# Cosine-similarity attention on one core: norm sums of later pairs attached one turn earlier, with new orders on three engines

## The chip, the core and the metric

The kernel runs on one core of a Trainium2 chip. The metric is the device time of one execution in microseconds. The core has five engines that run on their own and meet at semaphores: TensorE (PE in the profile, with its weight loads as PEld), VectorE (DVE), ScalarE (ACT), GpSimd (POOL) and SyncE (SP), which issues nearly all DMAs here. Each engine works through a list of instructions of its own.

## The reference

```
batch, heads, seq, dim = 8, 12, 512, 64          # Q, K, V in float32, tau = 0.1
Q_norm = Q / (norm(Q, axis=-1) + 1e-10)
K_norm = K / (norm(K, axis=-1) + 1e-10)
scores = einsum('bhqd,bhkd->bhqk', Q_norm, K_norm) / tau
weights = exp(scores - max(scores, -1));  weights /= sum(weights, -1) + 1e-10
out = einsum('bhqk,bhkd->bhqd', weights, V)
```

There are 96 heads. For each, the rows of Q and K are scaled to length one, a 512 x 512 matrix of scores is formed, its exponential is taken, and the weighted mean of the rows of V goes out. The kernel leaves the maximum away, as scores of unit vectors are bounded.

## The kernel before

The 96 heads are worked on as 48 **pairs**, numbered 0 to 47; the work on one pair in the steady state is a **turn**. For each pair s the function `pair` and its inner `rest` add small operations to a list, each with a name, an engine and the operations that it needs. The names and lines that matter:

- **Squares** `("SQ", s, 0)` (line 366): GpSimd squares all of Q and K of the pair into bfloat16. A few early ones are split (lines 254 to 357).
- **Norm sums** `("SSQ", s, w)` (line 395): TensorE adds up the squares with eight matmuls against the identity matrix, once for Q (w = 0) and once for K. They write into spare columns, from 320 on, of one of the two PSUM banks in which value products stand. Because of this a norm sum is *attached* to one half of the value products of an earlier pair, (i, h): it runs behind the last value group of that half, the reciprocal of that half waits for it too, and the next value products in the bank wait until its result has been read. Lines 209 to 229 choose the attachment: they go through the pairs in the order of a due time, `due_red`, and give each the first free half whose slot is not before it.
- **Norm reduce** `("RED", s, 1)` (line 404): VectorE reduces the sums of a pair to 128 x 16 squared norms. Four pairs (35, 39, 43, 47) are reduced by VectorE straight from the squares (line 412).
- **Root** `("NEW", g, k)` (lines 437 to 467): pairs are grouped in ones, twos and, from pair 20 on, fours. For each group a chain of eight or nine small VectorE steps makes the inverse roots out of the squared norms. For the first groups ScalarE does it.
- **Scale** `("SCL", s, w)` (line 479): Q (w = 0) and K (w = 1) times the inverse root, to bfloat16. VectorE does all of Q and 30 of the pairs' K, GpSimd the others' K.
- **Transpose** `("TR", s, w)` (line 488, TensorE, four matmuls) and **copy** `("EVA", s)` (line 506, VectorE), which brings the transposed pair out of PSUM.
- **Score product** `("SCO", s, c)` (line 625): two matmuls of 512 columns for chunk c, 0 to 3, of the keys. There are two PSUM places, so a score product waits for the exponential two before it.
- **Exponential** `("EXP", s, c)` (line 649): ScalarE, 128 x 1024 elements. In pairs 33, 40 and 46 the last chunk is not done by ScalarE: VectorE (lines 567, 569) and GpSimd (six steps, lines 589 to 595) work it out as a polynomial.
- **Cast** `("VC", s)` (line 657): GpSimd turns V into bfloat16.
- **Value product** `("PV", s, h, i)` (line 674): four matmuls, eight such groups for a pair, one bank for each head h. **Reciprocal** (line 690) and **normalise** (line 692) on VectorE empty the bank, and the next pair's products of that head wait for it. Then SyncE stores the result. The last pair's products have lines of their own (708 to 725).

What order the engines follow is not worked out when the program is built. `ORDER` at the end of the file holds, for each engine, a list of operation numbers, written out: number n is the n-th operation that was added. `schedule` (line 33) turns the lists into programs. `run` (line 43) puts a wait in front of an operation for what it needs from other engines. The due times (`due_sq`, `due_red` and others), the kinds of operation and constants such as START and PERIOD come from the planner that once wrote the lists. In this file only the attachment of norm sums still depends on them.

Some numbers that are used later: 663 is the scale of pair 16's K on GpSimd, 768 and 845 the squares of pairs 19 and 21, 708, 674 and 1831 the casts of pairs 17, 16 and 47; 846 and 847 the norm sums of pair 21; 666, 820, 1069, 1150, 1212, 1255 and 1410 score products (16,0), (20,0), (27,1), (29,3), (31,0), (32,0) and (36,0); 931 and 1225 value products (23,0,0) and (31,1,0); 906 and 1198 the normalisations (22,0) and (30,1); 1333 the copy of pair 34, 1363 a transpose of pair 35; 1790 to 1795 the six polynomial steps of pair 46 on GpSimd.

## Time and profile before

| | |
|---|---|
| median of 3 runs | 190.72 us (190.54 to 191.19) |
| the profiled execution | 190.63 us |
| its span, first to last instruction | 188.7 us |
| TensorE busy | 180.1 us, 95% |
| ScalarE busy | 181.0 us, 96% |
| VectorE busy | 167.8 us, 89% |
| GpSimd busy | 167.5 us, 89% |
| granted TensorE clock, mean | 0.997 |
| moved between HBM and the core | 50.79 MB |

The profile shows one execution. A row of its groups names line, engine and operation, what is written and read, the shapes, a count, busy time, the mean of one in ns, and the idle time of the engine ahead of it with what ended it. The chain of waits goes back from the last instruction, at each step to what released it. A timeline lists the instructions of one engine by start and length, neighbours of one kind merged; a bracket behind a row is idle time ahead of it. In a merged row the length runs from the first start to the last end. Instructions of an engine overlap by their pipelines, so that the start of the next is a better measure of a price than the length of one.

### The profile page before, as it was taken

What the parts mean: (1) busy time and instruction counts of PE and PEld (TensorE: products, weight loads), DVE (VectorE), ACT (ScalarE), POOL (GpSimd) and SP (SyncE); (2) the same over time, 40 slices, a digit from 0 to 9 for tenths busy, and PEclk for the clock granted to TensorE, in tenths of its full rate; (3) what the DMA queues carried; (4) which work ended last, traced back from release to release, by engine and by line L of the source; (5) the groups of instructions that cost most, each with busy time, mean ns of one, the idle gap of its engine ahead of it and who ended that gap; (6) DMA issues with size and microseconds to landing.
All of it is one profiled execution on the core that took longest, in us unless ns stands there. A gap on an engine that the chain in (4) does not pass through costs nothing.

```text
span 188.7 us, 7244 instructions
## 1 busy us (share of the span) xinstructions
PE 180.1 (95%) x3009; PEld 117.3 (62%) x3009; DVE 167.8 (89%) x539; ACT 181.0 (96%) x209; POOL 167.5 (89%) x143
## 2 busy tenths in 40 slices
PE   7899999999999999999999999999999999899993
PEld 2456666666666676677666665666577556455662
DVE  2788999999999988997979999999999999999654
ACT  5799999999999999999999999999999999999992
POOL 3699899979899899299999998989999999998980
PEclk9999999999999999999999999999999999999998
DMA  4999999999999998999999998974999540113335
GB/s 151 331 350 351 348 357 330 285 326 362 382 380 379 302 287 263 273 347 361 379 380 344 297 307 283 293 221 148 280 376 348 158 162 13 46 63 108 111 115 168
DMA packets 52448, 50.79 MB, mean 269 GB/s; under 512 B 3136, under 2 KB 52416, under 8 KB 52416
## 3 DMA queue, kind: packets, MB, share of 16 engines
q1 hardware_dynamic: 51984, 50.02, 80.7%
q8 instruction: 23, 0.38, 0.8%
q10 hardware_dynamic: 432, 0.33, 0.5%
q14 instruction: 9, 0.07, 0.1%
HBM read 37.75 MB, written 12.58 MB: 267 GB/s over the span
## 4 chain that ended last, share of the span: by engine, by line
PE 67%; DVE 16%; ACT 12%; DMA 1%; issue 1%; POOL 0%; DVEq 0%
PE oops L674 23%; PE scps L625 23%; ACT et L649 12%; PE tps L488 10%; PE oops L395 9%; DVE ob L692 3%; DVE qt L506 3%; DVE qn L479 2%; DMA qk<-in_K_dram 1%; DVE rd L690 1%; DVE nps L437 1%; DVE xp L567 1%; DVE nps L404 1%; DVE xz L569 1%; DVE xs L260 1%
## 5 line engine op out<-in xcount | busy, mean ns | idle before, releaser
L649 ACT ACTIVATE et<-scps 128x1024 bf16<-128x1024 f32 (+1 forms) x190 | 174.6, 1049 | 0.8 <-PE scps L625 0.4
L366 POOL TENSOR_TENSOR sq<-qk 128x1024 bf16<-128x1024 f32 x44 | 82.7, 1893 | 1.0 <-DMA qk<-in_K_dram 1.0
L625 PE MATMUL scps<-qt 64*128 64x512 bf16 x378 | 74.5, 386 | 1.3 <-ACT et L649 0.7
L674 PE MATMUL oops<-vb,et 128*128 128x65 bf16 x1504 | 74.5, 194 | 0.8 <-DVE ob L692 0.2
L674 PEld LDWEIGHTS oops<-vb,et 128*128 128x128 bf16 x1504 | 56.1, 98 | 30.6 <-issue 18.1
L479 DVE TENSOR_TENSOR qn<-qk,nps 128x512 bf16<-128x512 f32 x77 | 50.7, 676 | 0.6 <-ACT nps L429 0.6
L692 DVE TENSOR_TENSOR ob<-oops,rd 128x256 f32<-128x256 f32 x94 | 38.9, 418 | 1.3 <-DVE rd L690 0.2
L488 PE MATMUL tps<-ident,qn 128*128 128x128 bf16 x376 | 33.8, 220 | 0.8 <-DVE ys L437 0.4
L506 DVE COPY qt<-tps 128x1024 bf16<-128x1024 bf16 x47 | 32.1, 682 | 0.7 <-PE tps L488 0.5
L395 PE MATMUL oops<-sq,ident 128*128 128x64 bf16 x688 | 31.0, 193 | 0.5 <-POOL sq L357 0.5
L657 POOL TENSOR_SCALAR vb<-vf 128x512 bf16<-128x512 f32 x48 | 29.3, 626 | 0.3
L488 PEld LDWEIGHTS tps<-ident,qn 128*128 128x128 bf16 x376 | 21.6, 98 | 10.6 <-issue 4.3
L395 PEld LDWEIGHTS oops<-sq,ident 128*128 128x128 bf16 x688 | 24.3, 98 | 6.0 <-issue 4.3
L625 PEld LDWEIGHTS scps<-qt 64*128 64x128 bf16 x378 | 18.2, 92 | 14.7 <-ACT et L649 2.4
L479 POOL TENSOR_TENSOR qn<-qk,rk 128x512 bf16<-128x512 f32 x17 | 17.7, 1042 | 8.0 <-DVE rd L690 4.1
L690 DVE RECIPROCAL rd<-oops 128x4 f32<-128x4 f32 x94 | 15.8, 174 | 7.0 <-PE oops L674 4.6
L404 DVE TENSOR_REDUCE nps<-oops 128x16 f32<-128x128 f32 x40 | 11.4, 286 | 2.7 <-PE oops L395 2.6
L437 DVE SCALAR_TENSOR_TENSOR nps<-nps,ys 128x32 f32<-128x32 f32 (+3 forms) x48 | 8.3, 192 | 0.5
L590 POOL TENSOR_TENSOR xw<-xw,xz 128x1024 f32<-128x1024 f32 x3 | 7.1, 2356 | 0.3
L595 POOL TENSOR_TENSOR xz<-xz,xw 128x1024 f32<-128x1024 f32 x3 | 7.1, 2354 | 0.2
L590 POOL TENSOR_TENSOR xw<-xz 128x1024 f32<-128x1024 f32 x3 | 5.7, 1894 | 1.0 <-DVE xz L569 1.0
L590 POOL TENSOR_TENSOR et<-xw,xp 128x1024 bf16<-128x1024 f32 x3 | 6.4, 2126 | 0.2
(62 smaller groups left out, 75.2 us busy)
## 6 DMA issues: line engine op xcount, KB each, us to landing
vf<-in_V_dram SPq DMA_DIRECT2D x48, 256.0 KB, 6.1
qk<-in_Q_dram SPq DMA_DIRECT2D x47, 256.0 KB, 4.9
qk<-in_K_dram SPq DMA_DIRECT2D x47, 256.0 KB, 6.2
out_dram<-ob SPq DMA_DIRECT2D x47, 256.0 KB, 3.9
qk<-in_Q_dram SPq DMA_DIRECT2D x2, 128.0 KB, 2.6
qk<-in_K_dram ACTq DMA_DIRECT2D x2, 128.0 KB, 2.8
out_dram<-ob SPq DMA_DIRECT2D x1, 128.0 KB, 1.8
out_dram<-ob ACTq DMA_DIRECT2D x1, 64.0 KB, 1.7
```

The costliest lines, as they stand in the source:

```text
L366: lambda e: e.tensor_tensor(out=sqf, in0=data, in1=data, op=ALU.mult))
L395: last = e.matmul(out=o_ps[bank][:, at : at + 64], lhsT=ident[:, :], rhs=sq[iqs][:, 8 * w : 8 * w + 8, 8 * k : 8 * k + 8], start=(k == 0), ...
L479: lambda e, w=w, r=r: e.tensor_tensor(out=qn[iqn][:, w].rearrange("p t h d -> p h t d"), in0=qk[iq][:, w].rearrange("p h (t d) -> p h t d" ...
L488: last = e.transpose(t_ps[:, w, t, :], qn[iqn][:, w, t].rearrange("p h d -> p (h d)"), ident[:, :])
L506: lambda e, ws=ws: e.tensor_copy(out=qt[iqt][:, ws, :, :].rearrange("p w t x -> p (w t x)"), in_=t_ps[:, ws, :, :].rearrange("p w t x -> p ...
L590: mul = lambda o, x, y: lambda e: e.tensor_tensor(out=o, in0=x, in1=y, op=ALU.mult)
L625: last = e.matmul(out=sc_ps[:, 2 * b + h, :], lhsT=qt[iqt][64 * h : 64 * h + 64, 1, c, :], rhs=qt[iqt][64 * h : 64 * h + 64, 0, :, :], sta ...
L649: lambda e, c=c, b=b, hs=hs: e.activation(out=et[iet][:, c, hs[0] : hs[-1] + 1, :], in_=sc_ps[:, 2 * b + hs[0] : 2 * b + hs[-1] + 1, :], f ...
L657: return e.tensor_scalar(out=out, in0=in_, scalar1=1.0, scalar2=1.0, op0=ALU.mult, op1=ALU.mult)
L674: last = e.matmul(out=o_ps[h][:, 65 * t : 65 * t + 65], lhsT=et[iet][:, c, h, 128 * t : 128 * t + 128], rhs=vb[:, iq, c, h, :], start=(i = ...
L690: lambda e, hs=hs, grid=grid: e.reciprocal(out=rd[io][:, hs, :], in_=grid[:, :, :, DIM]))
L692: lambda e, hs=hs, grid=grid: e.tensor_tensor(out=ob[io][:, hs], in0=grid[:, :, :, 0:DIM], in1=rd[io][:, hs, :].unsqueeze(3).to_broadcast( ...
```

## The change

No operation is added or removed. Three things change.

- `due_sq` becomes 3 us earlier for pairs from 20 on (`M_MORE`, `MORE_FROM`). In the program this moves attachments: the norm sums of pairs 20 to 46 (all that TensorE does there; pair 19 stays) hang on value products one turn earlier than before. Those of pair 23, for example, on the first half of pair 15 in place of pair 16.
- The kinds of the root steps get names by group size (`half2`, `new4` and so on), under which the planner knew longer durations. The program doesn't use kinds.
- The lists of GpSimd, VectorE and TensorE are new: 96 of 139, 416 of 539 and 589 of 770 places hold another operation than before. The planner delayed operations at random when it made them. The lists of SyncE and ScalarE, and thus all DMAs and all exponentials, are unchanged.

The diff, with all of GpSimd's list and those lines of the other two in which the operations named above stand:

```diff
--- before.py
+++ after.py
@@ -201,7 +201,7 @@
 
     def due_sq(s):
         g = group[s]
-        return START + PERIOD * first[g] - 7.6 + (1.9 if g in NORM_ON_ACT else 0) - 3.43 * (first[g] + sizes[g] - 1 - s) - slack(s, M_SQ)
+        return START + PERIOD * first[g] - 7.6 + (1.9 if g in NORM_ON_ACT else 0) - 3.43 * (first[g] + sizes[g] - 1 - s) - slack(s, M_SQ) - (M_MORE if s >= MORE_FROM else 0)
 
     def due_red(s):
         return due_sq(s) + 2.0
@@ -464,7 +464,7 @@
                 needs = [("NEW", g, j) for j in after[k]] if k else reds + (free[1] if K_ON_DVE else [])
                 if 6 <= k < 8:
                     needs += free[k - 6]
-                P.add(("NEW", g, k), "dve", "new", TF - 4.9 - slack(s, M_NEW) + (M_STEP * (k - 7) if s > 8 else 0.23 * k), needs, step)
+                P.add(("NEW", g, k), "dve", ("half" if k >= 6 else "new") + str(sizes[g]), TF - 4.9 - slack(s, M_NEW) + (M_STEP * (k - 7) if s > 8 else 0.23 * k), needs, step)
 
         if s in off_of:
             P.add(("UNIT", s), "dve", "new", TF - 3.0, [("NEW", g, 6)], lambda e: e.tensor_scalar(
@@ -774,6 +774,7 @@
 START, PERIOD = 7.5, 3.62
 M_SQ, M_NEW, M_SCL, M_VC = 5, 2, 2, 2
 M_STEP = 0.23
+M_MORE, MORE_FROM = 3, 20
 TR_AT = (0.2, 1.2)
 PV_AT = (1.1, 2.1, 2.2, 2.3, 3.1, 3.2, 3.3, 4.1)
 
@@ -811,72 +812,72 @@
         "1730 1764 1809 1838 1852 "
     ),
     "pool": (
-        "0 1 14 2 4 22 35 69 106 107 144 145 50 188 231 89 265 308 127 171 237 248 342 214 384 418 291 314 367 "
-        "461 478 325 401 495 433 538 572 614 444 544 521 555 691 648 725 631 768 708 597 674 802 663 845 879 785 "
-        "751 913 947 828 774 990 930 885 896 1024 1058 862 1092 1007 1135 1169 1041 973 996 1118 1075 1203 1186 "
-        "1237 1280 1325 1152 1220 1359 1107 1308 1141 1209 1392 1435 1469 1263 1375 1252 1342 1364 1503 1536 1590 "
-        "1302 1303 1304 1305 1306 1307 1441 1658 1475 1624 1691 1418 1519 1734 1452 1486 1813 1573 1641 1768 1607 "
-        "1596 1567 1568 1569 1740 1570 1571 1572 1831 1717 1796 1751 1674 1790 1791 1792 1793 1794 1795 "
+        "2 0 1 14 4 22 35 69 106 107 144 145 50 188 231 89 265 127 171 308 248 237 342 214 384 314 367 418 291 "
+        "461 478 401 325 444 495 433 538 572 614 544 648 555 597 725 521 691 631 802 663 768 845 879 751 913 674 "
+        "947 774 708 785 990 896 885 1024 973 1058 862 828 1092 930 1135 1007 1169 1118 996 1203 1237 1186 1041 "
+        "1075 1280 1152 1325 1107 1141 1209 1359 1308 1392 1220 1263 1435 1342 1375 1252 1364 1469 1503 1536 1590 "
+        "1302 1303 1304 1305 1306 1441 1307 1475 1658 1624 1418 1691 1486 1734 1573 1519 1452 1813 1768 1674 1596 "
+        "1717 1567 1568 1569 1740 1570 1571 1572 1796 1751 1607 1641 1790 1791 1792 1793 1794 1795 1831 "
     ),
     "dve": (
...
-        "964 994 905 1138 906 1030 998 907 908 939 1028 1172 1062 940 1064 1032 941 942 1206 982 1096 1097 1098 "
...
-        "1331 1163 1438 1195 1164 1196 1362 1504 1197 1333 1505 1198 1472 1396 1397 1229 1230 1398 1231 1232 1399 "
...
+        "1028 964 994 873 874 1030 998 905 1172 906 907 1062 908 1064 1032 1206 1096 1097 1098 939 941 1099 942 "
...
+        "1301 1163 1362 1164 1504 1472 1195 1505 1197 1396 1198 1397 1196 1329 1398 1231 1399 1232 1400 1401 1404 "
+        "1229 1402 1230 1333 1407 1274 1366 1405 1403 1275 1439 1409 1272 1539 1273 1473 1443 1508 1319 1320 1317 "
...
     "pe": (
...
-        "562 563 804 623 662 664 625 598 803 599 627 600 601 769 629 770 696 602 666 698 603 604 668 605 847 670 "
-        "632 633 634 846 672 635 881 739 700 636 880 702 637 741 638 704 675 676 677 678 639 706 914 915 743 679 "
...
-        "755 783 756 991 992 820 852 850 757 822 758 759 786 787 824 788 789 1026 826 790 1025 791 854 792 884 "
...
-        "904 931 932 933 969 934 1171 1170 971 935 936 1031 999 937 1029 1001 974 975 976 938 1003 977 1204 1205 "
...
-        "1067 1106 1108 1069 1042 1043 1044 1045 1071 1046 1281 1047 1073 1048 1282 1049 1142 1110 1140 1112 1076 "
...
-        "1077 1078 1079 1327 1114 1326 1080 1116 1081 1082 1083 1176 1144 1174 1146 1123 1210 1148 1208 1124 1150 "
-        "1125 1119 1120 1253 1178 1251 1121 1126 1122 1180 1288 1286 1182 1153 1157 1154 1184 1296 1158 1212 1155 "
...
-        "1221 1332 1259 1194 1222 1223 1261 1224 1470 1471 1290 1225 1226 1292 1227 1228 1294 1264 1365 1363 1334 "
...
-        "1538 1316 1537 1371 1442 1440 1373 1343 1344 1345 1346 1591 1592 1347 1410 1412 1348 1474 1476 1349 1350 "
...
+        "560 664 623 662 561 625 562 598 599 600 601 627 770 769 563 629 846 847 666 698 696 668 602 603 604 670 "
...
+        "816 758 783 752 759 753 754 820 755 1025 1026 822 850 852 824 786 787 788 789 826 1060 1059 854 790 791 "
...
+        "903 967 904 1029 931 969 932 1031 933 971 934 1205 1204 999 935 936 937 938 1001 1063 1065 1003 978 974 "
...
+        "1067 1013 1014 1015 1142 1069 1140 1042 1043 1071 1044 1045 1326 1073 1327 1046 1047 1048 1049 1110 1174 "
...
+        "1253 1121 1251 1122 1150 1394 1393 1178 1288 1286 1180 1153 1125 1126 1182 1296 1154 1155 1184 1156 1436 "
+        "1437 1157 1212 1158 1159 1299 1214 1187 1188 1216 1189 1160 1190 1218 1470 1255 1471 1191 1192 1193 1257 "
+        "1194 1259 1332 1225 1226 1261 1221 1227 1228 1222 1223 1290 1330 1224 1292 1268 1269 1270 1271 1294 1264 "
+        "1363 1365 1334 1265 1266 1336 1267 1408 1406 1338 1538 1537 1313 1340 1442 1440 1367 1309 1314 1310 1369 "
+        "1311 1312 1315 1316 1371 1592 1591 1347 1373 1348 1349 1350 1410 1343 1476 1344 1412 1345 1380 1474 1346 "
...
```

89 rows, old and new, of the table ORDER are left out of this document.

## The prediction

> **What bounds the kernel now.** I read the page first: busy shares, the chain that ended last, the costliest group.
>
> ```profile
> span 188.7 us, 7244 instructions
> PE 180.1 (95%) x3009; PEld 117.3 (62%) x3009; DVE 167.8 (89%) x539; ACT 181.0 (96%) x209; POOL 167.5 (89%) x143
> ...
> PE 67%; DVE 16%; ACT 12%; DMA 1%; issue 1%; POOL 0%; DVEq 0%
> ...
> L649 ACT ACTIVATE et<-scps 128x1024 bf16<-128x1024 f32 (+1 forms) x190 | 174.6, 1049 | 0.8 <-PE scps L625 0.4
> ```
>
> No engine has room: ScalarE's exponentials and TensorE fill the span between them, and VectorE and GpSimd are at 89%. Next I asked how evenly the exponentials follow each other, by the timeline of ScalarE cut at several places (start, length, count).
>
> ```profile
> 11.84 70.25 ACT L649 ACTIVATE et<-scps 128x1024 bf16<-128x1024 f32 x76
> ...
> 37.47 7.50 ACT L649 ACTIVATE et<-scps 128x1024 bf16<-128x1024 f32 x8
> ...
> 40.18 5.71 ACT L649 ACTIVATE et<-scps 128x1024 bf16<-128x1024 f32 x6
> ...
> 81.04 60.82 ACT L649 ACTIVATE et<-scps 128x1024 bf16<-128x1024 f32 x65
> ...
> 142.28 41.65 ACT L649 ACTIVATE et<-scps 128x1024 bf16<-128x1024 f32 x45 [0.42 <-PE scps L625]
> ```
>
> Of the stretches from 37.47 and from 40.18 the second ends one exponential later (45.89 against 44.97), so three of them lie between the two starts: 2.71 / 3 = 0.903 us. That is the pace when nothing is late. From 11.84 to 81.04 there are 75 starts, 0.923 us each; from 81.04 to 142.28 65 starts, 0.942; from there to the end of the row, at 183.93, 45 in 41.65, about 0.92. Against 0.903 the three stretches lose 1.5, 2.5 and 0.9 us. So **4.9 us is all that any order of the work could win**, half of it between 81 and 142 us, and an exponential that comes late is hardly made up, since the pace has only 0.02 us of room in each.
>
> What the exponentials wait for is the score product of TensorE. The prices of its groups come from the chain of waits:
>
> ```profile
> 30.75 0.32 PE scps L625 x2
> ...
> 49.34 0.35 PE oops L674 x8
> ...
> 51.16 0.33 PE tps L488 x4
> 52.04 0.34 PE oops L395 x8
> 53.07 0.47 PE oops L674 x12
> ...
> 55.93 0.57 PE oops L395 x16
> 56.82 0.55 PE tps L488 x8
> 57.70 0.59 PE oops L674 x16
> ```
>
> Value products (L674) in fours: 0.35, 0.47, 0.59 for two, three, four groups, thus 0.12 a group and 0.11 for the change to a score product behind them. A norm sum (L395, eight matmuls) is 0.57 - 0.34 = 0.23, a transpose group 0.22, a score product 0.32. One pair of heads has four scores, eight value groups, two transposes and two norm sums: 1.28 + 0.44 + 0.96 + 0.44 + 0.46 = 3.58 us, against 4 x 0.903 = 3.61 for its exponentials. **TensorE and ScalarE run at the same rate**; neither can wait for long without the end moving.
>
> ```profile
> 82.00:100.00 18.00, 17.87 (x328) 12.36 (x325) 15.29 (x47) 18.00 (x21) 17.99 (x15) 1.00 1.08 372
> 100.00:118.00 18.00, 17.41 (x302) 11.40 (x298) 17.23 (x58) 17.90 (x20) 17.16 (x15) 1.00 0.94 303
> 118.00:142.00 24.00, 23.52 (x397) 15.48 (x396) 23.49 (x66) 23.83 (x26) 22.81 (x15) 1.00 0.84 266
> ```
>
> In this table by stage (length, then busy TensorE, weight load, VectorE, ScalarE, GpSimd, granted clock) VectorE has 2.7 us free in 82 to 100 and 0.5 us in 118 to 142: there it is the third bound.
>
> **The change, part by part.** The new names of the root steps' kinds (half2, new4) are planner's words; the program that is emitted doesn't read them, so they cost 0. What acts is the attachment (norm sums of pairs 20 to 46 hang on the value products of one turn earlier, same count of matmuls) and the three lists; SyncE's and ScalarE's lists, the DMAs too, stand as they were. Nothing is added or removed; the sum is made of waits that appear and go.
>
> *T1, TensorE's work comes earlier.* I counted, in both lists, the groups ahead of the same score product. Ahead of 820 (pair 20) the new list has two value groups more, 0.24 us. Ahead of 1069 (pair 27) two norm sums and one transpose more: 0.46 + 0.22 = 0.68. Ahead of 1150 (pair 29): two transposes, four value groups, 0.92. Ahead of 1212 (pair 31): four norm sums, one value group, 1.04. Ahead of 1255 (pair 32): one norm sum, 0.23; ahead of 1410 (pair 36) one value group less, -0.12. TensorE had 0.13 and 0.59 us of idle in the two stages, so these scores come up to 1.0 us later. By pair 36 the work is given back, and what the old order lost until then (2.5 us) takes up part. Between 0 and +1.0; I take +0.5.
>
> A page speaks here: the Trainium skill, "TensorE: Matmul & The Clock Gate", section "Back-to-back issue gap", gives about 81 ns a matmul for a stream of weight load and matmul pairs at 128 columns. By that the 16 matmuls of one pair's norm sums (64 columns) would cost up to an estimated 1.3 us, and T1 for two pairs 2.6. The rows above give 0.46 for the 16, 29 ns each, at a granted clock of 1.00, and 55 ns each in the transposes at 128 columns (0.22 / 4); the trace does not agree, and the rows decide.
>
> *T2, GpSimd waits earlier.* Scale 663 (keys of pair 16) now stands ahead of the squares 768 and of the casts 708 and 674.
>
> ```profile
> 60.13 1.89 POOL L366 TENSOR_TENSOR sq<-qk 128x1024 bf16<-128x1024 f32 x1
> 62.81 1.04 POOL L479 TENSOR_TENSOR qn<-qk,rk 128x512 bf16<-128x512 f32 x1 [0.79 <-DVE rk L437]
> 63.81 3.74 POOL L366 TENSOR_TENSOR sq<-qk 128x1024 bf16<-128x1024 f32 x2
> 67.52 1.21 POOL L657 TENSOR_SCALAR vb<-vf 128x512 bf16<-128x512 f32 x2
> ...
> 80.31 1.04 POOL L479 TENSOR_TENSOR qn<-qk,rk 128x512 bf16<-128x512 f32 x1 [3.83 <-DVE rd L690]
> ```
>
> It came to the scale at 62.02 and waited 0.79 us for the root. With 1.87 + 2 x 0.6 = 3.07 us less ahead it comes at 58.95 and waits 3.86, as the root itself stands about where it was. Behind it now go 768, then 845 (squares of pair 21), which ends at 62.81 + 1.00 + 2 x 1.87 = 67.55, where it ended 65.68. Its norm sums (846, 847) stood behind score 666, the first of them at 68.94; now both stand ahead of 666, with 0.46 us for the two, so near 67.1.
>
> ```profile
> 67.58 0.39 PE L625 MATMUL scps<-qt 64*128 64x512 bf16 x2
> ...
> 68.94 0.40 PE L395 MATMUL oops<-sq,ident 128*128 128x64 bf16 x8
> ```
>
> So TensorE waits some 0.4 us; bounds 0 (if TensorE is already late by that) and 1.9 (all of GpSimd's delay). The delay ends at the long wait before 80.31. +0.4.
>
> *T3, normalisations later.* On VectorE 906 (normalise pair 22) now has a norm reduce, two scales and a copy more ahead of it.
>
> ```profile
> 97.56 0.18 DVE L690 RECIPROCAL rd<-oops 128x4 f32<-128x4 f32 x1 [0.87 <-PE oops L395]
> 97.66 0.27 DVE L404 TENSOR_REDUCE nps<-oops 128x16 f32<-128x128 f32 x1
> 97.83 0.41 DVE L692 TENSOR_TENSOR ob<-oops,rd 128x256 f32<-128x256 f32 x1
> 98.17 0.68 DVE L479 TENSOR_TENSOR qn<-qk,nps 128x512 bf16<-128x512 f32 x1
> 98.76 0.68 DVE L506 COPY qt<-tps 128x1024 bf16<-128x1024 bf16 x1
> ...
> 98.55 0.66 PE L674 MATMUL oops<-vb,et 128*128 128x65 bf16 x16
> ```
>
> Start to start a reduce takes 0.17, a scale 0.59, a copy 0.60: 0.17 + 1.18 + 0.60 = 1.95 us later. The value product 931, which needs the bank that 906 empties, is the second group of the row at 98.55, so at 98.67, 0.43 behind 906's end (98.24); it moves back by two norm sums and a transpose, 0.68. Late by 1.95 - 0.68 - 0.43 = 0.84, less the 0.87 that VectorE idled ahead of 97.56, if it can fill it. Between 0 and 0.84; the same shape stands at pairs 23 to 25, with the same lateness, so it counts once. +0.3. Behind the waiting product stand the scores, that is ScalarE.
>
> *T4, the root of the first group of four late pairs.* Here VectorE has nothing free.
>
> ```profile
> 131.69 0.42 PE L674 MATMUL oops<-vb,et 128*128 128x65 bf16 x8 [0.20 <-DVE ob L692]
> ...
> 130.05 0.66 DVE L506 COPY qt<-tps 128x1024 bf16<-128x1024 bf16 x1
> ...
> 131.22 0.41 DVE L692 TENSOR_TENSOR ob<-oops,rd 128x256 f32<-128x256 f32 x1
> ```
>
> Value product 1225 already waited for 1198 with no margin. The new list brings 1225 up by four value groups, two scores with their changes and a transpose (0.48 + 0.86 + 0.22 = 1.56); 1198 comes up by a normalisation (0.33), a copy (0.60) and a scale (0.59), less a reduce and a root step (0.17 + 0.26, the step bounded by the reduce's length), 1.09. Late by 0.47. Copy 1333 goes behind the root's steps as well and the transposes 1363 wait for it. Between 0 and 1.2; +0.6.
>
> *T5, what goes.* The 0.42 us before 142.28 has one norm sum and more ahead of it cleared: -0.4. And the new list spaces the scores more evenly: summing what lies between neighbours over 0.903 gives 9.9 us in the old list, 8.4 in the new. Most of either is smoothed by running ahead; between 0 and -1.5, I take -0.6, since the three stretches lost 4.9 of the 9.9.
>
> Sum: 0.5 + 0.4 + 0.3 + 0.6 - 0.4 - 0.6 = **+0.8 us**. The profiled execution took 190.63 us with a span of 188.7 (1.9 outside, untouched); it lies 0.09 under the median 190.72. So 191.4 for an execution like that one, and 191.5 against the median.
>
> **Rivals.** *A, it gets faster:* moving the sums up fills VectorE's 2.7 free us in 82 to 100 and relieves 118 to 142, so that stretch runs at the pace of the first: 65 x (0.942 - 0.923) = 1.2 us less, 189.5. For it: VectorE's 98% there. Against: T1, T3. It decides when norm reduces that stood behind 118 us are done before 100. *B, nothing to see:* the new waits fall on what was lost anyway, 190.7. For it: the old order already lost 2.5 us there. *C, GpSimd's tail* (slower by more):
>
> ```profile
> 126.95 1.89 POOL L590 TENSOR_TENSOR xw<-xz 128x1024 f32<-128x1024 f32 x1 [0.60 <-DVE xz L569]
> ...
> 172.25 1.89 POOL L590 TENSOR_TENSOR xw<-xz 128x1024 f32<-128x1024 f32 x1 [0.45 <-DVE xz L569]
> ...
> 181.36 2.12 POOL L590 TENSOR_TENSOR et<-xw,xp 128x1024 bf16<-128x1024 f32 x1
> ...
> 183.54 0.74 PE L674 MATMUL oops<-vb,et 128*128 128x65 bf16 x16
> ```
>
> From 126.95 GpSimd goes on to 183.48 with hardly a gap, and the value products at 183.54 start 0.06 us behind it. Every delay of the first of these steps therefore reaches the end, and the new list puts cast 1831 (pair 47's values, 0.6 us) behind the last of them, ahead of the last products. If the first starts 1.0 late (T1's full amount, through the products that feed it) and the cast adds up to 0.6, the end is 1.6 later, plus half of the forecast's 0.8 elsewhere: 192.7. It decides once the delay at 126.95 passes about 0.5 us. Against it: 0.6 us of idle ahead of 126.95 covers GpSimd's own share.
>
> **How the numbers follow.** Forecast 0.37 (190.9 to 192.2 by itself), A 0.22, B 0.27, C 0.14. About 0.3% (0.57 us) is what a measurement of this kernel can tell from no change, so same is 190.15 to 191.29. Of the forecast 0.30 lies above and 0.07 within; of B 0.20 within, 0.03 below, 0.04 above. Faster 0.25, same 0.27, slower 0.48. The range goes down to A with 0.2 of grace, 189.3, and up to C with 0.5 for T2's upper bound, 193.2.
>
> **What would show it.** T1: exponentials of pairs 27 to 31 start about 0.5 us later against the first one, with TensorE busy. T2: a GpSimd wait of over 3 us near 59, and TensorE behind squares near 67. T3, T4: weight loads of L674 waiting on L692 near 99 and 130. T5: the 0.42 before 142 gone. C: a cast as GpSimd's last instruction with the last products behind it. The forecast is wrong if the stretch from 81 to 142 falls to 0.93 a start or under, or if the three stretches keep their paces.

## The result, and the profile after

| | before | after |
|---|---|---|
| median | 190.87 us (22 runs, 190.42 to 193.4) | 189.66 us (22 runs, 189.3 to 191.9) |
| ratio of the times | 1 | 0.9934 (95% interval 0.9912 to 0.9955) |
| the profiled execution | 190.63 us | 189.83 us |

The change makes the kernel 0.66% faster, 1.21 us in the medians. I had forecast 191.5 us, slower. In the runs further below, the profile of relief_late is of an execution 2.7 us longer than the median of that kernel; only what happens in it after pair 16 is used.

From the page of the changed kernel:

```profile
span 188.0 us, 7242 instructions
...
PE 178.4 (95%) x3009; PEld 117.4 (62%) x3009; DVE 167.4 (89%) x539; ACT 179.9 (96%) x209; POOL 167.3 (89%) x143
...
PE 68%; ACT 12%; POOL 10%; DVE 5%; DMA 2%; issue 1%; SPq 0%; DVEq 0%; POOLq 0%
...
L649 ACT ACTIVATE et<-scps 128x1024 bf16<-128x1024 f32 (+1 forms) x190 | 173.6, 1080 | 1.2 <-PE scps L625 1.0
```

The busy times are nearly those of before; in the chain that ended last VectorE's share went from 16% to 5%, and GpSimd's from 0 to 10%. The timeline of ScalarE in the changed kernel (start, length, count, idle time ahead):

```profile
12.27 51.54 ACT L649 ACTIVATE et<-scps 128x1024 bf16<-128x1024 f32 x56
63.99 119.10 ACT L649 ACTIVATE et<-scps 128x1024 bf16<-128x1024 f32 x129 [0.17 <-PE scps L625]
183.39 1.15 ACT L640 ACTIVATE et<-scps 128x512 bf16<-128x512 f32 x3 [0.30 <-PE scps L625]
```

Before, the row that began at 81.04 ended in a gap of 0.42 us at 142; here 129 exponentials follow each other without a gap. The last of them is some 1.1 us long, so 128 starts fall into about 118.0 us, 0.922 us each. That is the pace that before held up to 81 us (0.923) and lost from 81 to 142 (0.942). The same 65 exponentials that took 61.24 us from there take 59.79 in the changed kernel, 0.920 each.

Busy time by stage in the changed kernel, in the columns of the table in the prediction:

```profile
82.00:100.00 18.00, 18.00 (x322) 12.27 (x322) 16.49 (x50) 18.00 (x21) 18.00 (x18) 1.00 1.08 371
100.00:118.00 18.00, 17.71 (x320) 12.14 (x317) 17.63 (x60) 17.92 (x21) 17.62 (x17) 1.00 1.00 325
118.00:142.00 24.00, 23.52 (x388) 15.17 (x387) 22.91 (x66) 24.00 (x27) 23.09 (x15) 1.00 0.86 274
```

VectorE works 1.20 us more between 82 and 100 (15.29 before) and 0.58 us less between 118 and 142 (23.49). The start of the root steps shows the same. These are the first steps of the chains of pairs 28 to 31, 32 to 35 and 36 to 39, in VectorE's timeline of before:

```profile
104.26 0.23 DVE L441 TENSOR_SCALAR ys<-nps 128x64 int32<-128x64 int32 x1
...
115.37 0.22 DVE L441 TENSOR_SCALAR ys<-nps 128x64 int32<-128x64 int32 x1
...
131.88 0.23 DVE L441 TENSOR_SCALAR ys<-nps 128x64 int32<-128x64 int32 x1
```

and of after:

```profile
101.86 0.23 DVE L441 TENSOR_SCALAR ys<-nps 128x64 int32<-128x64 int32 x1
...
113.50 0.21 DVE L441 TENSOR_SCALAR ys<-nps 128x64 int32<-128x64 int32 x1
...
128.87 0.20 DVE L441 TENSOR_SCALAR ys<-nps 128x64 int32<-128x64 int32 x1
```

They come 2.40, 1.87 and 3.01 us earlier, while the exponentials up to pair 36 come at most 0.9 earlier in the same two profiles. So the roots have gained a lead. What that does to TensorE stands in the list of waits (what waited, for what: us in total, times, longest) from 82 to 143 us. Before:

```profile
PEld oops L674 <- DVE ob L692: 2.7, 9, 0.5
PEld oops L674 <- DVE nps L437: 0.7, 3, 0.2
```

After:

```profile
PEld oops L674 <- DVE ob L692: 1.1, 4, 0.4
PEld scps L625 <- ACT et L649: 1.5, 5, 0.6
```

The first row is weight loads of value products that wait for a normalisation, 2.7 us before and 1.1 after; the second row of after has TensorE waiting for ScalarE (0.2 us before), that is running ahead of it.

Weight loads overlap with matmuls, so such a row isn't all loss, and it leaves out what waits for a copy. The loss can be read more directly from the starts on TensorE. I call it a wait where the step from one group to the next is over 0.04 us longer than the median step of its kind and the group starts right behind the operation on another engine that it needs; what the step is too long is the loss. Between score products (22,0) and (37,0) that is ten waits for VectorE before the change, 2.02 us in total, about half of it for normalisations (0.99) and half for copies (1.03, of which 0.60 near 117.8 us alone). After the change one of 0.20 is left. Waits for ScalarE rise from 0.23 to 0.81 in the same stretch; there is none for GpSimd in either.

**A replay of TensorE's list.** To part what TensorE's own order costs from what it waits for, I priced the list by steps from start to start: score product 0.32, value group 0.12, transpose and norm sum 0.23, 0.095 for the change to a score product (the prediction has nearly the same from its rows). A score product waits until the exponential two before it has ended (1.1 us from its start), a value group for its exponential, and exponentials follow at 0.903 us at best, 0.45 behind their score product. This is an estimate of where the exponentials would be if VectorE and GpSimd were never late. What the profile shows beyond it I call waits. Their level hangs on the third place of the prices (with exactly 0.120 for a value group it is 3.83 and 2.51 at pair 46, in place of the 2.78 and 1.50 below); what they fall by hardly does (1.32 in place of 1.28). All starts are counted from the first exponential of pair 3, so that the first loads, which land up to 0.5 us apart in most of these profiles, drop out.

```
start of the first exponential      order, less before's       waits
of pair                           24     31     36     46     24    31    36    46
before                             0      0      0      0    0.92  1.94  2.20  2.78
after                          +0.21  +0.68  +0.14  -0.09    0.42  0.56  0.75  1.50
```

The new list of TensorE costs 0.68 us at pair 31 and has given it back by pair 37. The waits fall by 1.38 us at pair 31, 1.45 at pair 36. Order and waits together are -1.37 at pair 46; in the profile the last of all normalisations ends 1.25 earlier, counted in the same way, and the medians differ by 1.21.

### The profile page after: what moved, and what is told of

It is laid out like the page before. It is cut to its first block, busy times and chain, and to the rows that moved or that the text cites. A ratio compares the mean times of both kernels' runs of the same rounds, so it can differ in the third digit from the quotient of the medians.

```text
span 188.0 us, 7242 instructions
## 1 busy us (share of the span) xinstructions
PE 178.4 (95%) x3009; PEld 117.4 (62%) x3009; DVE 167.4 (89%) x539; ACT 179.9 (96%) x209; POOL 167.3 (89%) x143
## 4 chain that ended last, share of the span: by engine, by line
PE 68%; ACT 12%; POOL 10%; DVE 5%; DMA 2%; issue 1%; SPq 0%; DVEq 0%; POOLq 0%
PE oops L674 24%; PE scps L625 24%; ACT et L649 11%; PE oops L395 10%; PE tps L488 10%; POOL xw L590 2%; POOL sq L366 2%; DMA qk<-in_Q_dram 2%; POOL vb L657 2%; POOL xz L595 1%; POOL et L590 1%; POOL qn L479 1%; DVE ob L692 1%; DVE qt L294 1%; DVE xp L567 1%
## 5 line engine op out<-in xcount | busy, mean ns | idle before, releaser
L674 PE MATMUL oops<-vb,et 128*128 128x65 bf16 x1504 | 75.6, 194 | 0.5 <-DVE ob L692 0.3
L674 PEld LDWEIGHTS oops<-vb,et 128*128 128x128 bf16 x1504 | 56.9, 98 | 28.7 <-issue 20.0
L479 DVE TENSOR_TENSOR qn<-qk,nps 128x512 bf16<-128x512 f32 x77 | 51.4, 677 | 0.7 <-ACT nps L429 0.6
L488 PE MATMUL tps<-ident,qn 128*128 128x128 bf16 x376 | 32.8, 220 | 0.7 <-DVE qn L479 0.7
L395 PE MATMUL oops<-sq,ident 128*128 128x64 bf16 x688 | 29.3, 193 | 0.0
L395 PEld LDWEIGHTS oops<-sq,ident 128*128 128x128 bf16 x688 | 23.5, 98 | 6.4 <-issue 5.2
L690 DVE RECIPROCAL rd<-oops 128x4 f32<-128x4 f32 x94 | 16.4, 177 | 7.2 <-PE oops L674 3.7
```

Source lines behind the costliest of these rows:

```text
L395: last = e.matmul(out=o_ps[bank][:, at : at + 64], lhsT=ident[:, :], rhs=sq[iqs][:, 8 * w : 8 * w + 8, 8 * k : 8 * k + 8], start=(k == 0), ...
L479: lambda e, w=w, r=r: e.tensor_tensor(out=qn[iqn][:, w].rearrange("p t h d -> p h t d"), in0=qk[iq][:, w].rearrange("p h (t d) -> p h t d" ...
L488: last = e.transpose(t_ps[:, w, t, :], qn[iqn][:, w, t].rearrange("p h d -> p (h d)"), ident[:, :])
L674: last = e.matmul(out=o_ps[h][:, 65 * t : 65 * t + 65], lhsT=et[iet][:, c, h, 128 * t : 128 * t + 128], rhs=vb[:, iq, c, h, :], start=(i = ...
L690: lambda e, hs=hs, grid=grid: e.reciprocal(out=rd[io][:, hs, :], in_=grid[:, :, :, DIM]))
```

## The experiments

All times are ratios to the kernel before on the same chip, with the 95% interval; "at pair 36" is the start of its first exponential, counted from pair 3, less the same in the profile of before.

**The new lists up to a point: new_to_100, new_to_125, new_to_150.** Theory R was that the gain is TensorE's waits for VectorE next to the root steps; A is the rival of the prediction, E that it lies outside 82 to 142 us.

```diff
 # on TensorE, VectorE, GpSimd: what the changed kernel starts by 100 us
 # (its first 405, 303, 80 numbers), then the rest in before's order
-M_MORE, MORE_FROM = 3, 20
+M_MORE, MORE_FROM, MORE_TO = 3, 20, 30     # 37 and 44 in the other two
```

> The new lists of TensorE, VectorE and GpSimd (with the new attachment of the norm sums in them, pairs 20 to 30) for everything that the changed kernel had started by 100 us, then the rest in the old order. Theory R (the change gains by taking away TensorE's waits for VectorE's copies and normalisations between about 105 and 136 us, next to the root steps of the groups of four): little is gained yet, 0.2 us faster to 0.3 us slower than before. Theory A (the norm sums, done earlier, fill VectorE's idle time from 82 to 100 us, and that is the gain): at least half of it is here, 0.5 us or more faster. Theory E (the gain lies outside 82 to 142 us, in the first exponentials or the last products): if in the head, 0.5 or more faster; if in the tail, 0.0.

> The same with the cut at 125 us (norm sums up to pair 37). R: the waits near 117, 119 and 121 us (0.60, 0.12, 0.17) are gone, those near 131 and 136 are left: 0.4 to 0.8 us faster than before. A: all of the gain is here, and as much at new_to_100 already. E: no difference to new_to_100.

> The same with the cut at 150 us (norm sums up to pair 44); only the last pairs go in the old order. R: all of what the exponentials gained by pair 36 (0.9 us against the kernel before), and the old tail, in which the changed kernel lost 0.6 us against it: 1.2 us faster than before, 189.4 to 189.7 where before is 190.9, as fast as the changed kernel or up to 0.5 faster. A: about as the changed kernel, 0.7 to 1.2 faster. E (tail): no faster than before.

Measured: 0.9961 (0.9934 to 0.9987), 0.9952 (0.9923 to 0.998), 1.0024 (0.9983 to 1.0066). In the profiles the exponentials are 0.28, 0.61 and 1.31 us earlier at pair 36, and up to its cut the exponentials of each kernel start where those of the changed one do, to 0.01 us. So the gain is made bit by bit from pair 22 to pair 36, not in the head and not in the tail: E falls, and A, which wanted half of it by 100 us, has 0.28 of 1.31 in the profile. By the times alone A could stand: new_to_100 is 0.74 us faster in them (0.25 to 1.26), more than its profile. The single jumps of the last section, which come with before's first part, are in that ratio and could be the difference; this isn't shown. What speaks against A more clearly is sums_alone and relief_late, below. The profile of the third kernel loses its 1.3 at the seam, and most of its times are longer still, at a lower granted clock (last section). Its waits from 148 to 160 us:

```profile
PE oops L674 <- DVE ob L692: 1.4, 1, 1.4
...
ACT et L649 <- PE scps L625: 1.0, 1, 1.0
```

There the new prefix ends and the old list goes on: normalisation (36,1) stands behind four scales, a copy and a polynomial step. This single one that comes late costs 1.26 us up to pair 39.

**The end: after_tail.**

```diff
   pe (of the changed kernel):
-  1801 1798 1799 1802 1800 1827 1803
+  1798 1799 1827 1801 1802 1800 1803      # 1827: score product (47,3)
   pool:
-  1790 1791 1792 1793 1794 1795 1831
+  1831 1790 1791 1792 1793 1794 1795      # 1831: cast of pair 47
```

> The changed kernel with two places of the end altered: TensorE issues the last score product (47,3) ahead of the value product (46,1,0), which waits 0.6 us for a normalisation, and GpSimd casts the values of pair 47 ahead of the six polynomial steps of pair 46 and not behind them. By R the changed kernel throws away 0.5 to 0.6 us here: 0.5 us faster than the changed kernel, 1.5 to 1.8 faster than before. By E (the gain is in the tail): slower than the changed kernel, or the same.

Measured 0.9896 (0.9854 to 0.9938), 189.44 us (6 runs, 189.24 to 189.83) against the changed kernel's 189.66 in other runs. TensorE's timeline at the end of the changed kernel, then of this one:

```profile
182.10 0.92 PE L674 MATMUL oops<-vb,et 128*128 128x65 bf16 x20 [0.29 <-DVE ob L692]
```

```profile
181.67 0.39 PE L625 MATMUL scps<-qt 64*128 64x512 bf16 x2
...
183.27 0.66 PE L708 MATMUL oops<-vb,et 128*128 128x65 bf16 x16 [0.43 <-DVE ob L692]
```

The last exponentials do come 0.57 us earlier in relation to the others, but the last value products then wait 0.43 for the normalisation of pair 46, and the end lies where the changed kernel has it (the last normalisation 1.20 against 1.25 us earlier than before). The two are not told apart, and the 0.5 us of theory R don't come.

**Single places: score36_up, transposes_up, both_edits, norms_up, hand_edits.** If the waits are the cause, taking them away in the old lists should win as much.

```diff
   score36_up, pe:                  transposes_up, pe (and the copies 1177 1211 1254 on dve alike):
-  1346 1591 1592 1347 1410         1116 1081 1082 1083 1176 1144 1174
+  1346 1410 1591 1592 1347         1116 1176 1174 1081 1144 1082 1083
   norms_up, dve, one of five:
-  1197 1333 1505 1198
+  1197 1198 1333 1505
```

> The kernel before with one place altered: TensorE issues score product (36,0) behind the value group (34,0,3) and not behind the two norm sums of pair 41 and one more value group that stand there (0.58 us of work). Theory R2 (the gain is made at two places where TensorE's list of before puts too much ahead of a score product: this one, and the transposes of pairs 30 to 33): counted from pair 3, exponentials of pair 36 and later come 0.45 to 0.55 us earlier, and the time falls by 0.3 to 0.55 us. Theory A (the norm sums, done earlier, fill VectorE's idle time from 82 to 100 us): no sum is earlier, so less than 0.2 us.

> The kernel before with the transposes of pairs 30 and 31 and what lies between score products (28,3) and (30,2) in another order on TensorE, and on VectorE the copies of pairs 30, 31, 32 each ahead of up to four root steps, a normalisation or a scale that stood before them. R2: the waits of 0.60, 0.12 and 0.17 us near 117, 119 and 121 shrink to under 0.3 together, exponentials from pair 31 on come 0.35 to 0.5 us earlier, counted from pair 3; the time falls by 0.3 to 0.5 us. A: no sum is earlier, less than 0.2 us.

> The two edits of score36_up and transposes_up in one kernel, the rest as before. R2: they add up, 0.8 to 1.0 us earlier from pair 36 on and to the end, most of what the change wins (1.2 us in the medians). A: less than 0.3 us.

> The kernel before with VectorE's list alone altered at five places (near 90, 94, 107, 130 and 135 us): normalisations (20,1), (21,1), (25,0), (30,1), (32,1) and the copy of pair 27 stand ahead of the root step, norm reduce, scale or copy that stood before them. No norm sum moves. Theory R3 (the changed kernel wins where its lists put what TensorE waits for ahead of VectorE's root steps and scales; the earlier norm sums by themselves cost): the six waits of TensorE (0.08, 0.20, 0.15, 0.15, 0.27, 0.26 us) shrink to under 0.3 together, exponentials from pair 36 on come 0.3 to 0.7 us earlier, counted from pair 3. If VectorE's order is of no weight (the gain was TensorE's own order): less than 0.15 us.

Measured: 1.0022 (0.9996 to 1.0048), 1.0000 (0.9979 to 1.0021), 0.9998 (0.9976 to 1.002), 1.0008 (0.9983 to 1.0032). None has a gain that the times show. In the profile score36_up wins 0.57 us at pair 36, as expected, and loses 0.76 before the pair is over. Its timeline of ScalarE:

```profile
119.23 25.19 ACT L649 ACTIVATE et<-scps 128x1024 bf16<-128x1024 f32 x27
144.89 3.08 ACT L649 ACTIVATE et<-scps 128x1024 bf16<-128x1024 f32 x3 [0.46 <-PE scps L625]
```

The gap has moved from 142.28 to 144.89: the groups that the score product was moved past stand ahead of a later one. The replay, by prices alone, has -0.55 and then +0.64. transposes_up keeps 0.26 us to the end, both_edits -0.71 at pair 36 and +0.06 at pair 37. norms_up removes the waits that it aimed at, and the sum of these rows stands where it stood:

```profile
PEld oops L674 <- DVE ob L692: 2.7, 11, 0.3
...
PEld oops L674 <- DVE nps L404: 0.5, 1, 0.5
```

2.7 us in eleven waits in place of nine, and the wait for a norm reduce has gone from 0.2 to 0.5. Read from the starts as above, TensorE's waits for VectorE fall only from 2.02 to 1.79 us. Theories R and R2, in which single waits or two places hold the gain, fall. So does R3, in as much as it takes these six waits one by one for the gain. hand_edits is norms_up, transposes_up and casts_first (below) in one kernel:

> The edits of norms_up, casts_first and transposes_up in one kernel; all norm sums stand where they stood before. R3 with L: 0.6 to 1.1 us faster than before, exponentials from pair 37 on 0.5 to 0.9 us earlier counted from pair 3. If the earlier norm sums are needed for the gain (theory N): under 0.3 us faster.

0.9988 (0.9964 to 1.0012), 0.20 us earlier from pair 37 on. It is under 0.3, as N has it, but it doesn't show that the sums are what lacks.

**The sums alone: sums_alone, sums_spread.**

```diff
 # pe: each pair of norm sums right behind the last group of its new half
-  903 967 904 931 932 933 969 934 1171 1170 971       # 1170, 1171: pair 30
+  903 967 904 1171 1170 931 932 933 969 934 1204 1205 971   # 1204, 1205: pair 31; and so on to pair 41
 # dve: its reduce behind the reciprocal of that half
-  907 908 939 1028 1172 1062 940
+  907 1172 908 939 1206 1028 1062 940                 # 1206: pair 31's reduce
-M_MORE, MORE_FROM = 3, 20
+M_MORE, MORE_FROM, MORE_TO = 3, 30, 41
```

> The kernel before with the norm sums of pairs 30 to 41 alone one turn earlier (their squares are ready by then), each right behind the last value group that it is attached to, its reduce behind the reciprocal of that half; nothing else moves. R2: the sums of pair 41 leave the place ahead of score product (36,0), so 0.4 to 0.5 us is won there; the transposes of pairs 30 to 33 stand as they were, so the loss near 117 to 121 stays within 0.2 us of its size: 0.3 to 0.6 us faster in all. A: both losses go, 0.8 us or more faster. My forecast's first term (TensorE's work comes earlier and holds up the scores of pairs 27 to 31): exponentials of pair 31 come 0.5 us later than before.

Measured 1.0044 (1.0026 to 1.0062), slower. Its timeline of ScalarE:

```profile
100.08 7.54 ACT L649 ACTIVATE et<-scps 128x1024 bf16<-128x1024 f32 x8 [0.19 <-PE scps L625]
107.93 14.05 ACT L649 ACTIVATE et<-scps 128x1024 bf16<-128x1024 f32 x15 [0.31 <-PE scps L625]
122.37 62.38 ACT L649 ACTIVATE et<-scps 128x1024 bf16<-128x1024 f32 x67 [0.40 <-PE scps L625]
```

The gap at 142 is gone, as both theories had it, and three new ones stand behind score products (24,2), (26,2), (30,1), each of which has both sums of a pair (30, 33, 36) and three or four value groups right ahead of it: +0.74 us at pair 31, +0.79 at the end. This is the cost that T1 speaks of, though at other places than in the changed kernel and for norm sums alone. Nor do the roots gain a lead: counted from pair 3, the three chains start 0.41 us later, 0.44 earlier and 0.44 later than before, where the changed kernel has them 2.83, 2.30 and 3.45 earlier, as the rest of VectorE's list stands as it was. By the replay the order costs 1.50 at pair 46 and the waits fall to 2.07 from 2.78. So the earlier sums do take waits away, but less than they cost where they stand. In sums_spread they stand apart:

> As sums_alone (the kernel before, norm sums of pairs 30 to 41 one turn earlier), but on TensorE the sums are set apart from each other, each in a place where little else lies between two score products, and seven score products go one to three places up. Theory W (two parts that add: what TensorE's own list puts ahead of each score product, priced with the profile's 0.32, 0.12, 0.23 us, and TensorE's waits for VectorE): against the kernel before the list of sums_alone costs 1.50 us by these prices and this one 0.61; the waits fell from 2.78 to 2.07 us in sums_alone and should stay there. So 0.9 us faster than sums_alone and within 0.3 us of the kernel before, counted from pair 3 to pair 46. Theory N0 (the sums' place alone decides, not the list around them): as sums_alone, 0.8 us slower than before.

Measured 1.0037 (1.0014 to 1.0059), no faster than sums_alone. The order costs 0.61, as priced, but the waits rose to 3.00 by pair 46, and from pair 37 to 46 the exponentials start within 0.04 us of where sums_alone has them. Waits from 82 to 143 us:

```profile
PEld oops L674 <- DVE ob L692: 2.7, 8, 0.8
...
PE oops L674 <- DVE ob L692: 0.7, 2, 0.5
```

Theory W, order and waits as parts that simply add, falls: what TensorE won by its order, it lost again waiting for VectorE, whose list is the same in both kernels.

**The sums back in the new lists: sums_back.**

```diff
-M_MORE, MORE_FROM = 3, 20
+M_MORE, MORE_FROM, MORE_TO = 3, 20, 29
 # pe, dve: sums and reduces of pairs 30 to 46 one turn down;
 # root steps, some scales, transposes 28 behind them
 # pool: five places, scales of K of pairs 28, 29, 31, 32, 35
```

> The changed kernel with the norm sums of pairs 30 to 46 back one turn, attached as before the change, and what depends on them (reduces, root steps, some scales, pair 28's transposes) moved down its lists only as far as needed; all else as in the changed kernel. R3 (moved alone in the old order the sums cost 0.8 us): between the changed kernel's time and 0.8 us faster than that. Theory N (the new order can place its transposes early only because the sums are early): 0.4 us or more slower than the changed kernel, with waits of TensorE for copies at pairs 28 to 33.

Measured 1.0622 (1.0573 to 1.0671), 203.1 us. Its timeline of ScalarE has, among others:

```profile
110.48 7.44 ACT L649 ACTIVATE et<-scps 128x1024 bf16<-128x1024 f32 x8 [1.99 <-PE scps L625]
...
125.00 15.14 ACT L649 ACTIVATE et<-scps 128x1024 bf16<-128x1024 f32 x16 [2.99 <-PE scps L625]
```

Each of the two stands behind a chain of roots that starts 3.6 and 5.3 us later than in the changed kernel, counted from pair 3: scale, transpose, copy and score product wait in turn. N was right that this costs more than 0.4 us and that TensorE waits at pairs 28 to 33, but not in what it waits for: the two longest waits there, 1.21 us at pair 28 and 2.61 at pair 32, are transposes behind scales, the second behind one of GpSimd, whose list this kernel changes too. The granted clock was lower as well, 0.975 to 0.992 in its six executions. It is no price of the sums by themselves, since an order made for late sums might be better than this one; it shows that the new lists use the lead which the early sums give.

**VectorE's amount of work: relief_late, relief_early, before_filled, after_filled.**

```diff
 # relief_late, in RED of pairs 35 and 39
-  in_=sq[iqs][:, 8 * w : 8 * w + 8, :]
+  in_=sq[iqs][:, 8 * w : 8 * w + 8, 0:32]
 # relief_early: scales (23,0) (24,0) (24,1) (25,0) over t = 0, 1 of four
 # before_filled, after_filled: two scales issued once more into spare[i]
```

> The kernel before with VectorE's four reduces of squares of pairs 35 and 39 over 32 of 64 elements in place of all (this leaves out half of their sums): about 0.3 us less each, 1.2 us less VectorE work between 110 and 131 us. Lists as before. Theory A (VectorE's work, piled up between 100 and 142 us, sets the pace there, and the change wins by doing some of it before 100): exponentials of pair 36 and later 0.5 to 1.2 us earlier counted from pair 3, time 0.5 to 1.2 us less. Theory P (TensorE's own order sets the pace, VectorE only follows): less than 0.2 us.

> The control: the kernel before with four of VectorE's scales, (23,0), (24,0), (24,1), (25,0), over half of their elements (the other half is left out): about 0.3 us less each, 1.2 us less VectorE work between 85 and 97 us, where it idles 2.7 of 18 us. A: no use of more idle time there as long as the later work keeps its places in the list, less than 0.3 us faster. P: less than 0.2 us as well.

> The kernel before with two scales of VectorE, (23,0) and (24,1), issued once more into a spare tile: 1.2 us more VectorE work between 85 and 94 us. A: the idle time there takes most of it, 0 to 0.4 us slower. P: 0 to 0.2 us.

> The changed kernel with two scales of VectorE, (23,1) and (24,1), issued once more into a spare tile: 1.2 us more VectorE work between 86 and 93 us, where it idles less than in the kernel before. A: the gain of the change is used up, exponentials of pair 36 and later 0.6 to 1.2 us later than in the changed kernel, counted from pair 3. P: under 0.3 us later.

Measured: 0.9995 (0.9973 to 1.0017), 1.0002 (0.9969 to 1.0035), 1.0037 (1.0008 to 1.0067), 0.9937 (0.9917 to 0.9958). The stage table of relief_late:

```profile
100.00:118.00 18.00, 17.84 (x322) 11.94 (x319) 16.46 (x51) 17.90 (x20) 18.00 (x15) 1.00 1.00 330
118.00:142.00 24.00, 23.18 (x376) 14.87 (x375) 23.16 (x71) 23.96 (x27) 21.93 (x17) 1.00 0.77 246
```

VectorE is relieved of about 1.1 us there, and the exponentials win 0.10 us at pair 36, of which 0.02 are left at pair 44. From pair 31 to 37 TensorE waits 0.07 us for VectorE in place of 0.52, but 0.55 in place of 0.23 for ScalarE. With 1.2 us less work before 100, they win 0.20. The mere amount of VectorE's work is not what binds, and theory A falls in this form. The other two runs came out the other way round from what A expected. In before, which idles 2.7 us from 82 to 100, the 1.2 us more cost 0.60 us (the other 0.61 of that profile's delay is older, from pairs 4 and 12); in the changed kernel, which idles 1.5 us there, they cost 0.18. (Theory P, which wanted at most 0.2 us in before, has that wrong too.) The 0.60 is one wait. Value product (22,1,0) needs normalisation (21,1); in before it waits 0.20 us for it, in before_filled 0.80. TensorE's timeline of before, then of before_filled:

```profile
94.84 0.30 PE L674 MATMUL oops<-vb,et 128*128 128x65 bf16 x4
```

```profile
96.09 0.30 PE L676 MATMUL oops<-vb,et 128*128 128x65 bf16 x4 [0.73 <-DVE ob L694]
```

A bracket counts from the end of the work ahead, so it is smaller than the wait from start to start, and missing for the 0.20. The second of the two scales that are issued twice stands four places ahead of that normalisation, and a scale takes 0.59 us. The table of after_filled for the stage:

```profile
82.00:100.00 18.00, 17.92 (x324) 12.38 (x322) 17.27 (x52) 18.00 (x21) 18.00 (x18) 1.00 1.05 359
```

VectorE takes 0.78 us more in this stage, and TensorE is busy for 17.92 us of it in place of 18.00. **Idle time isn't slack**, at least here: where TensorE already waits for a result with no margin, a scale put ahead of that result cost its full length, whatever VectorE idled elsewhere in the stage. The changed kernel has no such wait there. This is one place in one pair of kernels, and the scales that are issued twice aren't quite the same in both ((23,0) and (24,1) in before, (23,1) and (24,1) in the changed kernel).

**The squares of pair 7: casts_first.**

```diff
-  231 89 265 308 127 171 237        # pool; 308: squares, 127 and 171: casts
+  231 89 265 127 171 308 237
```

> The kernel before with GpSimd's list altered at one place, near 19 us: the squares of pair 7 behind the casts of pairs 2 and 3, as in the changed kernel, and not ahead of them. Theory L (where the load for these squares lands late, the casts behind them hold up the value products of pair 2, and the time rises by 0.5 us and more in some executions): the profile has no delay of an exponential near pair 4, the median falls by 0.1 to 0.4 us, and the highest of the times is under 191.5. If L is wrong: times as before, up to 193 us.

Measured 1.0001 (0.9976 to 1.0025), times from 190.58 to 192.97. Its profile has no delay at pair 4, but the profile of before has none there either, and the spread is what it was. Theory L isn't borne out.

## Why the prediction was wrong

**What bounds the kernel** was right: TensorE and ScalarE at one rate, 2.5 us lost from 81 to 142, and the gain lies there. But I read the exponentials' pace and stopped. The list of waits for that stretch, with 2.7 us of weight loads behind normalisations, is the row that I didn't read, and 1.6 us of it went.

**T1** (+0.5) had about the right size as a cost of TensorE's own order: +0.68 by the replay at pairs 28 to 34. Its sign, exponentials of pairs 27 to 31 about 0.5 us late, didn't come: counted from pair 3 they are 0.18 us early at pair 28 and 0.69 at pair 31, as the waits fall by more. I also wrote that the work is given back by pair 36. It is, and with it the 0.42 us gap; at the end T1 and the first half of T5 together are -0.09. I had counted them as +0.5 and -0.4.

The prediction set a rule of the Trainium skill beside T1 (page "TensorE: Matmul & The Clock Gate", section "Back-to-back issue gap": about 81 ns a matmul for pairs of weight load and matmul at 128 columns). The rows of the changed kernel, at a granted clock of 1.00, say what those of before said:

```profile
67.48 0.64 PE L395 MATMUL oops<-sq,ident 128*128 128x64 bf16 x16
68.06 0.39 PE L625 MATMUL scps<-qt 64*128 64x512 bf16 x2
```

These are the norm sums of T2: 0.58 from start to start less 0.11 for the change, 0.47 for 16 matmuls of 64 columns, 29 ns each. The page's figure is for 128 columns; the rows nearest to that are the transposes of the prediction, at 55 ns each, and don't agree with it either.

**T2, T3, T4** (+0.4, +0.3, +0.6) failed: these +1.3 us of new waits are the step of the prediction that went wrong first. GpSimd's wait came, though of 2.00 us and not 3.86, since GpSimd comes to this scale 2.17 us earlier and not 3.07, and the root 0.95 us earlier and not where it was (counted from pair 3):

```profile
62.30 1.04 POOL L479 TENSOR_TENSOR qn<-qk,rk 128x512 bf16<-128x512 f32 x1 [2.00 <-DVE rk L437]
```

The squares behind it were done in time, and the norm sums at 67.48 have no idle time ahead of them in TensorE's timeline; score product 666 behind them is 0.03 us late. Value products 931 and 1225, which T3 and T4 had late by 0.84 and 0.47, don't wait in the profile of after. The step that failed is the same in all three: I moved one operation and left its partners at their old times. The lateness of 906 was counted from the four operations put ahead of it, but those start earlier too, by 1.5 to 6.1 us counted from pair 3, and the 0.87 us of idle time ahead of its reciprocal is down to 0.06, as T3's lower bound allowed. So 906 is 0.48 us late and not 1.95, and 931 is 0.17 late without a wait. 1198 and 1225 both come 2.7 us earlier. Where all lists are new, the old start times are no base for a difference.

**T5, second half** (-0.6) looked for the gain in the wrong place. I looked at how evenly TensorE's own list spaces the scores and took a share of 1.5 us. The evenness of that list is worth nothing at the end (order -0.09), while its waits for the other engines, for which I had no term at all except the 0.20 at 131.69, fell by 1.28 us by pair 46. Put together, by the replay: +1.3 for new waits that didn't come, 1.28 less for old waits that went and that I had put at nothing, against 0.41 that I had granted the order too much (T1 and T5 are -0.5 in the sum, and it is -0.09). That makes 2.17, from my +0.8 to the -1.37 at pair 46.

**Rival A** gave 189.5 and its stage numbers nearly came: 1.20 of the 2.7 us filled, 0.58 relieved. That the time came out near it is luck, as its reason did not hold: the sums moved up alone make the kernel slower (1.0044), 1.1 us less work for VectorE from 100 to 142 wins 0.10 at most, and no norm reduce that stood behind 118 us came before 100. **Rival B** had no new waits, which was right, but it let the old ones stand. **Rival C**'s cast is GpSimd's last instruction, as it said, and ends at 183.38; the first product that needs it, at 183.44, has no idle time ahead of it on TensorE. The lateness at 126.95 from which C would decide did not come either: that step starts 1.17 us earlier, counted from pair 3.

What is shown: the exponentials win their 1.3 us from pair 22 to 36, and in that stretch TensorE waits 1.8 us less for VectorE and 0.6 more for ScalarE; the gain is not to be had from the sums alone, from the single places that I tried, or from less work on VectorE at the two places where I took some away. No run takes all of these waits away and leaves the rest as it was. What stays open: whether the gain needs the sums one turn earlier, and which part of the new lists makes it. sums_alone says that the sums take 0.7 us of waits away and cost more; sums_back that the new lists as they stand can't do without their lead; no run had an order made anew for late sums.

## What to carry to other kernels

Where every engine follows a written list, price a new order as a whole: a wait taken away in one place came back in the next (0.57 us won and 0.76 lost within one pair), and a delay counted against old start times didn't come. Read the waits of the engine that bounds a stretch, in total and by releaser, before you judge its order. An engine's idle time alone doesn't tell what it can take on; ask how long its results lie ready before they are used.

## What the runs showed of the hardware

Between two kernels that share their lists up to some point, and whose profiles have none of the jumps named below, all starts on TensorE, VectorE and ScalarE up to there agree within 0.02 us, counted from pair 3, over 100 us and hundreds of waits (new_to_100, new_to_150 and after_tail against the changed kernel). GpSimd's don't: some differ by 0.1 to 1.5 us without the other engines showing it. What differs from run to run comes in single jumps: the first exponentials, mostly up to 0.5 us (2.1 in the profile of relief_late), and in some profiles with the old first part 0.1 to 0.5 us at pair 4 and 0.1 to 0.6 at pair 12. In score36_up GpSimd's squares waited for a load there:

```profile
20.43 1.89 POOL L366 TENSOR_TENSOR sq<-qk 128x1024 bf16<-128x1024 f32 x1 [1.15 <-DMA qk<-in_K_dram]
```

None of the profiles with the changed kernel's first part has such a jump, and the times of some of these kernels lie closer together (190.04 to 190.89 in 12 runs of new_to_100, 189.5 to 190.17 in 11 of after_filled) than those of before (190.36 to 193.69). new_to_150, with the same first part, spreads from 190.61 to 193.69, and there the long times go with a lower granted TensorE clock: three executions at 1.00 took 190.61 to 191.01 us, the other nine, at 0.979 to 0.991, 191.66 to 193.69. What lowers the clock there isn't shown. Nor is it the reason for all long times of before, of which some are at a clock of 1.00 (193.27 us). casts_first rules out the one place that I tried.
